# Hybrid attention layer: queries and keys transposed whole in f32 and split into two parts out of PSUM

## The chip, the cores and the metric

One core of one Trainium2 chip runs the whole layer in one launch. The metric is the device time of one execution in microseconds (us). The time before is the median of 3 runs; the profile comes from one further execution, whose own time stands beside its span below.

## What is computed

One decoder layer on x of 2048 tokens by 1024 channels, all in float32. Cut to what matters here:

```
hdn  = rmsnorm(x, norm_gain)
proj = hdn @ w_in                      # q,k,v,gate of mixer A and of mixer B
q, k = rope(rmsnorm_per_head(q)), rope(rmsnorm_per_head(k))
o_a  = banded_attention(q_a, k_a, v_a, 127, sinks)      # 8 heads, 2 key heads, window 128
o_b  = merge of three banded attentions at stride 1, 4, 16   # 8 heads
mixed = concat(o_a * silu(g_a), o_b * silu(g_b))
out  = x + mixed @ w_out
```

The scores are q·k over 64 channels per head. The gains of the per-head norm are large, so scores need nearly full float32 accuracy.

## The kernel before, in words

**Numbers in two parts.** TensorE multiplies in `float32r`, a format with a shorter mantissa than float32. So every operand x is held as a high part hi (x rounded to float32r) and a low part lo = x − hi, and a product is a sum of matmuls over parts: three for the projections (`mm3`, line 244), two for the scores (lines 590 and 591). Making the parts is elementwise work: hi is a copy on ACT with a float32r result, lo a subtraction on DVE or POOL.

**Stages.** `STAGES` lists eight passes over the sequence: four of kind B (two heads of mixer B each), two of kind A (four query heads and one key head of mixer A each) and two of kind O (half of the output columns each). Each pass goes over four blocks `sb` of 512 tokens, each block over two halves of 256 tokens, each half over two tiles `tt` of 128 tokens. Per tile, 24 matmuls of 128x384 (line 244) give queries, keys and values in a PSUM tile `pj`; per half, 24 (B) or 48 (A) of 128x256 give the gates.

**From projection to transposed queries and keys.** `norm_rope` (lines 405 to 431) squares and sums on ACT and DVE, multiplies by the rotary tables on DVE and adds on POOL (line 430); the result t1 has 128 tokens on the partitions. `norm_factors` computes the inverse norms on POOL (line 182). `norm_split` (lines 440 to 460) multiplies t1 by them on DVE (line 446) and writes a tile `hl` of both parts: high parts on ACT (lines 455, 456; the key's twice), low parts on POOL (lines 457, 458). `qk_transposes` (lines 462 to 503) then brings the heads' channels on the partitions with TensorE transposes of 128x128 float32r (lines 474, 484, 489, 490, 498) against the identity `idr`. In B a half takes ten of them in three PSUM tiles, in A twelve in four; each tile holds the high part of one head in one half of the partitions and its low part in the other, so that one matmul over 128 channels gives hi·k_hi + lo·k_hi, and a second one against `KL` (half of whose rows are zero) gives hi·k_lo. ACT copies the tiles out (lines 476, 477, 486, 492, 493, 501). In B, POOL copies the queries once more in another order (line 478) for the spill to memory that the dilated attention reads back.

**PSUM.** The transposes use the tile name `po`, which has two buffers. The same two serve the PV matmuls of the attention (lines 645, 735, 849) with their copies out (`ob` on ACT, then an addition on DVE, lines 566 to 570 and 737 to 740), the transposes of row statistics (lines 671, 877) and, in the first stage, lines 198 and 211.

**What sets the order.** A generator `proj` emits the projection; after each step the main loop emits attention steps from a queue `pending`, by cost numbers. The `finish` of a half (carry of the last keys, then `qk_transposes`) is deferred to the end of the second tile's matmuls of the next half. A scheduler then orders each engine's instructions with its own timeline, so the order in the program differs from the order in the text. Every engine runs its instructions in order: an instruction that waits holds up all behind it on that engine. DMAs are issued from SP.

**x and weights.** x arrives as `xs` and is split into `xh` (ACT, line 155) and `xl` (POOL or DVE, line 157) in groups of two 128-channel chunks; a half uses four groups, and there are `XB` = 6 buffers of each part. At a change of stage the next weights arrive as `stg` and are split on ACT (line 104) and DVE (line 105).

Of the kernel before, what the change touches and what calls it, by code (L numbers as in the profile page):

```python
# [21 lines left out]
XB = 6  # L22
# [11 lines left out]
def hybrid_layer(ctx, tc, xT, xn, x, wB, wA, wO, ng, gains, sinks, rot, masks, ident, out):  # L34
# [16 lines left out]
    idr = const.tile([128, 128], F32R, name="idr")  # L51
# [21 lines left out]
    def late_constants(part):  # L73
        if part == 0:
            nc.sync.dma_start(gt.rearrange("p a b c d -> p (a b c d)"),
                              bass.AP(tensor=gains.tensor, offset=gains.offset, ap=[[0, 128], [1, 512]]))
            return
        nc.sync.dma_start(idf, ident)
        nc.scalar.activation(idr, idf, AF.Copy)
# [166 lines left out]
    def proj(si, sb):  # L246
# [22 lines left out]
        for half in range(2):  # L269
# [66 lines left out]
            hls = norm_split(kind, nq, nk, t1s, fac)  # L336
            if si == 0 and hf < 7:
                rb_make(hf + 1)
            deferred.append(lambda half=half, hls=hls: finish(si, sb, half, hls))

    def finish(si, sb, half, hls):
# [3 lines left out]
        if half == 0 and sb > 0:  # L345
            pk, pl = K[si, sb - 1]
            for h in range(nk):
                nc.scalar.activation(KK[:, h, :, 0, :], f32(pk[:, h, :, 4, :]), AF.Copy)
            for h in range(nk):
                hs = slice(64 * h, 64 * h + 64)  # L350
                nc.scalar.activation(KL[hs, h, :, 0, :], f32(pl[hs, h, :, 4, :]), AF.Copy)
        yield from qk_transposes(si, sb, half, hls)
# [87 lines left out]
    def norm_split(kind, nq, nk, t1s, fac):  # L440
        nh = nq + nk
        n = nh * 64
        hls = []
        for tt, t1 in enumerate(t1s):
            t1v = t1[:, :n].rearrange("p (h d) -> p h d", d=64)
            nc.vector.tensor_tensor(t1v, t1v, fac[:, tt, :, None].to_broadcast([128, nh, 64]), op=OP.mult)  # L446
            hl = wk.tile([128, 11, 64], F32R, name="hl", bufs=2)
            k0 = 2 * nq
            if kind == "A":
                hi, lo = hl[:, 0:8:2, :], hl[:, 1:8:2, :]  # L450
            else:
                hi, lo = hl[:, 0:4:3, :], hl[:, 1:3, :]
            khi = hl[:, k0:k0 + 2 * nk, :].rearrange("p (h a) d -> p h a d", a=2)
            klo = hl[:, k0 + 2 * nk:k0 + 3 * nk, :]
            nc.scalar.activation(hi, t1v[:, :nq], AF.Copy)
            nc.scalar.activation(khi, t1v[:, nq:, None, :].to_broadcast([128, nk, 2, 64]), AF.Copy)
            nc.gpsimd.tensor_tensor(lo, t1v[:, :nq], f32(hi), op=OP.subtract)
            nc.gpsimd.tensor_tensor(klo, t1v[:, nq:], f32(khi[:, :, 0, :]), op=OP.subtract)
            hls.append(hl)
        return hls  # L460

    def qk_transposes(si, sb, half, hls):
        kind, _ = STAGES[si]
        KK, KL = K[si, sb]
        q = Q[si, sb]
        i0 = 2 * half

        for tt, hl in enumerate(hls):
            i = i0 + tt
            if kind == "B":  # L470
                blocks = [hl[:, 2 * b:2 * b + 2, :] for b in range(4)]
                pt = ps.tile([128, 4, 128], F32R, name="po", bufs=2)
                for b, a in enumerate(blocks):
                    nc.tensor.transpose(pt[:, b, :], a, idr)
                pv = f32(pt).rearrange("p h (r u) -> p h r u", u=32)
                nc.scalar.activation(q[0][:, :, i, :], f32(pt)[:, 0:2], AF.Copy)
                nc.scalar.activation(KK[:, :, :, i + 1, :], pv[:, 2:4], AF.Copy)
                nc.gpsimd.tensor_copy(q[1].rearrange("p h r (i u) -> p h r i u", u=32)[:, :, :, i, :],
                                      f32(q[0][:, :, i, :]).rearrange("p h (r u) -> p h r u", u=32))
                yield 230  # L480
            else:
                pt = ps.tile([128, 4, 128], F32R, name="po", bufs=2)
                for b in range(4):
                    nc.tensor.transpose(pt[:, b, :], hl[:, 2 * b:2 * b + 2, :], idr)
                for p in range(2):
                    nc.scalar.activation(q[p][:, :, i, :], f32(pt)[:, 2 * p:2 * p + 2], AF.Copy)
                yield 230
                pt = ps.tile([128, 4, 128], F32R, name="po", bufs=2)
                nc.tensor.transpose(pt[:, 0, :], hl[:, 8:10, :], idr)
                nc.tensor.transpose(pt[:64, 1, :], hl[:, 10, :], idr)  # L490
                pv = f32(pt).rearrange("p h (r u) -> p h r u", u=32)
                nc.scalar.activation(KK[:, 0, :, i + 1, :], pv[:, 0], AF.Copy)
                nc.scalar.activation(KL[:64, 0, :, i + 1, :], pv[:64, 1], AF.Copy)
                yield 110
        if kind == "B":
            pt = ps.tile([128, 2, 128], F32R, name="po", bufs=2)
            for tt, hl in enumerate(hls):
                nc.tensor.transpose(pt[:, tt, :], hl[:, 8:10, :], idr)
            for h in range(2):
                hs = slice(64 * h, 64 * h + 64)  # L500
                nc.scalar.activation(KL[hs, h, :, i0 + 1:i0 + 3, :].rearrange("p r i u -> p i r u"),
                                     f32(pt[hs]).rearrange("p i (r u) -> p i r u", u=32), AF.Copy)
            yield 110
# [60 lines left out]
    def evac_o(po, dst):  # L564
        ob = wk.tile([64, 512], F32, name="ob", bufs=1)
# [10 lines left out]
    def window_scores(si, sb, h, nb, l):  # L576
# [5 lines left out]
        for b in range(2):  # L582
            sc = ps.tile([128, 2, 256], F32, name="sc", bufs=2)
            for j in range(2):
# [4 lines left out]
                lw = KL[:, kh, :, k0:k0 + 2, :].rearrange("p r a u -> p a r u")  # L589
# [109 lines left out]
    def pair_units(si, sb, p, sc, osum, rows, final):  # L699
# [24 lines left out]
        def pv(b):  # L724
# [11 lines left out]
            ob = wk.tile([64, 512], F32, name="ob", bufs=1)  # L736
# [214 lines left out]
    pcost = {"B": 4 * 8 * 490 + 2 * 8 * 330 + 4 * 340, "A": 4 * 8 * 490 + 4 * 8 * 330 + 4 * 340, "O": 4 * 8 * 650}  # L951
# [88 lines left out]
```

## Time and profile before

| | |
|---|---|
| time, median of 3 runs | 1270.55 us (1269.44 to 1271.11) |
| profiled execution | 1271.72 us, of which the span of instructions 1269.9 us |
| mean granted TensorE clock | 0.970 |
| DVE busy | 867.5 us, 2288 instructions |
| ACT busy | 837.1 us, 2418 instructions |
| POOL busy | 685.3 us, 788 instructions |
| DMA | 220.98 MB, mean 174 GB/s |

How to read the profile's rows. A row of the grouped instructions has line, engine, operation, output<-inputs, shapes and count, then total busy us and mean ns of one, then the idle time of the engine just before these instructions and what ended most of it ("<-POOL hl L457 7.9": 7.9 us ended when POOL's line 457 had written hl). A row of the timeline has start, duration, engine, line, operation and count, and in brackets the idle time before it with what ended it. A row of the windows has the stretch, its length, the busy time of each engine (with instructions), the granted clock as a share of full speed, the DMA share and GB/s. Durations of matmuls overlap, so the pace of TensorE is read from differences of start times. PEld is the weight load that goes with each matmul.

### The profile page before, as it was taken

The numbers are of one execution on the slowest core, as the hardware profiler recorded it, in microseconds if no ns is written. First come the engines' busy times: TensorE is split into PE (matmuls) and PEld (weight loads), VectorE is DVE, ScalarE is ACT, GpSimd is POOL, SyncE is SP. The second block draws the span as 40 slices with busy tenths as digits, with TensorE's granted clock in tenths as the row PEclk, the third lists the DMA queues.
The fourth block names the chain that finished last, engine by engine and source line by source line (L and its number), as shares of the span: only waits on it lengthen the run. The fifth ranks groups of instructions, "written<-read, shape, count | busy, mean of one in ns | idle before, by whom it ended". The sixth has DMA issues, their size and how long they took to land. (4 is left out here: it accounts for less than half of the span.)

```text
span 1269.9 us, 25442 instructions
## 1 busy us (share of the span) xinstructions
PE 1179.8 (93%) x8328; PEld 1143.5 (90%) x8328; DVE 867.5 (68%) x2288; ACT 837.1 (66%) x2418; POOL 685.3 (54%) x788
## 2 busy tenths in 40 slices
PE   6898979988799898898998999999899999999899
PEld 6798979988699898898997999998799998999898
DVE  5666678776667677776877879888777868622221
ACT  6567777777668587676877767786776877513221
POOL 4876644566454755545676566673556565333122
PEclk9899989999999899898998999999899999999999
DMA  7454678776677776787866775555223235566551
GB/s 215 128 148 114 176 214 243 211 202 185 193 212 232 198 198 181 219 235 197 221 200 191 212 199 150 149 165 165 91 73 109 80 97 157 164 197 205 177 188 70
DMA packets 196883, 220.98 MB, mean 174 GB/s; under 512 B 34312, under 2 KB 143632, under 8 KB 196752
## 3 DMA queue, kind: packets, MB, share of 16 engines
q1 hardware_dynamic: 196752, 219.37, 59.2%
q8 instruction: 66, 1.08, 0.4%
q14 instruction: 65, 0.53, 0.1%
HBM read 164.44 MB, written 54.86 MB: 173 GB/s over the span
## 5 line engine op out<-in xcount | busy, mean ns | idle before, releaser
L244 PE MATMUL pj<-wh,xh 128*128 128x384 f32 (+1 forms) x1008 | 334.1, 334 | 18.6 <-ACT xh L155 6.7
L244 PE MATMUL pj<-wl,xh 128*128 128x384 f32 (+1 forms) x1008 | 334.9, 332 | 1.4 <-DVE wl L102 0.8
L244 PE MATMUL pj<-wh,xl 128*128 128x384 f32 (+1 forms) x1008 | 331.9, 331 | 1.1 <-POOL xl L157 0.8
L157 POOL TENSOR_TENSOR xl<-xs,xh 128x512 fp32r<-128x512 f32 x158 | 213.7, 1365 | 143.8 <-ACT xh L155 139.1
L155 ACT ACTIVATE xh<-xs 128x512 fp32r<-128x512 f32 x252 | 153.5, 627 | 115.8 <-PE pj L244 98.8
L244 PEld LDWEIGHTS pj<-wh,xh 128*128 128x128 f32 x1008 | 194.4, 193 | 22.4 <-ACT xh L155 7.1
L244 PEld LDWEIGHTS pj<-wl,xh 128*128 128x128 f32 x1008 | 194.6, 193 | 3.6 <-DVE wl L102 1.1
L244 PEld LDWEIGHTS pj<-wh,xl 128*128 128x128 f32 x1008 | 194.4, 193 | 3.5 <-DVE xl L157 1.3
L574 DVE TENSOR_TENSOR ptl<-pt,pth 128x512 fp32r<-128x512 f32 (+3 forms) x232 | 141.6, 619 | 42.2 <-ACT pth L573 40.2
L244 PE MATMUL pj<-xh,wgh 128*128 128x256 f32 x496 | 147.1, 297 | 10.7 <-DVE V L310 8.4
L244 PE MATMUL pj<-xh,wgl 128*128 128x256 f32 x496 | 145.3, 293 | 0.0
L244 PE MATMUL pj<-xl,wgh 128*128 128x256 f32 x496 | 144.7, 292 | 0.0
L573 ACT ACTIVATE pth<-pt 128x512 fp32r<-128x512 f32 (+3 forms) x232 | 123.1, 543 | 25.6 <-PE po L645 9.4
L430 POOL TENSOR_TENSOR t<-t,t 128x256 f32<-128x256 f32 (+1 forms) x96 | 79.2, 826 | 80.9 <-DVE t L421 57.2
L244 PEld LDWEIGHTS pj<-xh,wgh 128*128 128x128 f32 x496 | 97.7, 197 | 12.9 <-DVE V L310 5.8
L446 DVE TENSOR_TENSOR t<-t,fac 128x256 f32<-128x256 f32 (+1 forms) x96 | 76.9, 815 | 33.0 <-POOL fac L182 30.1
L244 PEld LDWEIGHTS pj<-xh,wgl 128*128 128x128 f32 x496 | 97.7, 197 | 0.8
L814 ACT ACTIVATE P<-P,scD 128x128 f32<-128x128 f32 (+3 forms) x128 | 71.6, 560 | 40.5 <-DVE scD L813 39.6
L244 PEld LDWEIGHTS pj<-xl,wgh 128*128 128x128 f32 x496 | 97.8, 197 | 0.4
L157 DVE TENSOR_TENSOR xl<-xs,xh 128x512 fp32r<-128x512 f32 x94 | 79.8, 859 | 20.2 <-ACT xh L155 19.8
L182 POOL TENSOR_TENSOR fac<-un,mhalf 128x8 f32<-128x8 f32 (+1 forms) x48 | 85.3, 1778 | 2.7
L599 ACT ACTIVATE P<-P,scA 128x256 f32<-128x256 f32 (+1 forms) x128 | 63.1, 495 | 23.4 <-DVE scA L598 23.0
(188 smaller groups left out, 3087.8 us busy)
## 6 DMA issues: line engine op xcount, KB each, us to landing
xs<-in_xT SPq DMA_DIRECT2D x94, 512.0 KB
xs<-mx SPq DMA_DIRECT2D x32, 512.0 KB
vd<-V SPq DMA_DIRECT2D x64, 128.0 KB
qd<-qc SPq DMA_DIRECT2D x32, 256.0 KB
TT<-tab SPq DMA_DIRECT2D x32, 256.0 KB
cv<-vd SPq DMA_DIRECT2D x32, 256.0 KB
cq<-qd SPq DMA_DIRECT2D x32, 256.0 KB
ck<-kd SPq DMA_DIRECT2D x64, 128.0 KB
```

The costliest lines, as they stand in the source:

```text
L155: nc.scalar.activation(h, f, AF.Copy)
L157: eng.tensor_tensor(l, f, f32(h), op=OP.subtract)
L182: nc.gpsimd.tensor_tensor(y, u, mhalf.to_broadcast([128, n]), op=OP.pow)
L244: nc.tensor.matmul(o, a, b, start=first and n == 0, stop=last and n == 2, skip_group_check=True)
L430: nc.gpsimd.tensor_tensor(t1[:, :n], t1[:, :n], t2[:, :n], op=OP.add)
L446: nc.vector.tensor_tensor(t1v, t1v, fac[:, tt, :, None].to_broadcast([128, nh, 64]), op=OP.mult)
L573: nc.scalar.activation(hi, pt, AF.Copy)
L574: nc.vector.tensor_tensor(lo, pt, f32(hi), op=OP.subtract)
L599: nc.scalar.activation(pd, pd, AF.Exp, bias=nb[i], scale=-1.0, accum_out=l[i])
L814: nc.scalar.activation(pd, pd, AF.Exp, bias=nb, scale=-1.0, accum_out=l)
```

## The change

- `hl` and `norm_split` go. `norm_scale` keeps only the DVE multiplication of t1 (line 441 of the changed kernel).
- The transposes take t1 itself, in float32 against `idf`, two heads (128 columns) at a time, two token tiles into one PSUM tile. A half of B has four transposes in one `po` tile, a half of A four of 128 columns in one tile and two of the key's 64 columns in another. `idr` goes.
- The parts are made on the way out of PSUM, on 64 partitions and 256 elements at a time: ACT copies hi, then DVE subtracts it from the PSUM tile and writes lo to the other half of the partitions. The key's hi is copied twice by ACT, its lo is one subtraction. In A the second pair of query heads is transposed after the copies of the first pair in the text, into the same tile.
- POOL's reordering copy in B stays, now two in a row per half. The carry of `KL` in A is two copies instead of one, and in A odd heads use the other plane of `KL`.
- `finish` yields once per half in B (436) and twice in A (436 and 218); the cost table `pcost` follows.
- `XB` goes from 6 to 7, and `ob` from one buffer to two.

```diff
-XB = 6
+XB = 7
...
-    def norm_split(kind, nq, nk, t1s, fac):
...
+    def norm_scale(nh, t1s, fac):
         for tt, t1 in enumerate(t1s):
...
             nc.vector.tensor_tensor(t1v, t1v, fac[:, tt, :, None].to_broadcast([128, nh, 64]), op=OP.mult)
-            hl = wk.tile([128, 11, 64], F32R, name="hl", bufs=2)
...
-            nc.scalar.activation(hi, t1v[:, :nq], AF.Copy)
-            nc.scalar.activation(khi, t1v[:, nq:, None, :].to_broadcast([128, nk, 2, 64]), AF.Copy)
-            nc.gpsimd.tensor_tensor(lo, t1v[:, :nq], f32(hi), op=OP.subtract)
-            nc.gpsimd.tensor_tensor(klo, t1v[:, nq:], f32(khi[:, :, 0, :]), op=OP.subtract)
...
+        def queries(tile, h, src):
+            a, b = (hi64, lo64) if h else (lo64, hi64)
+            o = tile[:, h, i0:i0 + 2, :]
+            nc.scalar.activation(o[a], src[a], AF.Copy)
+            nc.vector.tensor_tensor(o[b], src[a], f32(o[a]), op=OP.subtract)
+
+        if STAGES[si][0] == "B":
+            pt = ps.tile([128, 2, 2, 128], F32, name="po", bufs=2)
+            for b in range(2):
+                for tt, t1 in enumerate(t1s):
+                    nc.tensor.transpose(pt[:, b, tt, :], t1[:, 128 * b:128 * b + 128], idf)
+            for h in range(2):
+                queries(q[0], h, pt[:, 0])
+            pk = pt[:, 1].rearrange("p i (r u) -> p i r u", u=32)
+            for h, (a, b) in enumerate(((lo64, hi64), (hi64, lo64))):
+                nc.scalar.activation(keys(KK, h)[a], pk[a], AF.Copy)
+                nc.scalar.activation(keys(KK, h)[b], pk[a], AF.Copy)
+                nc.vector.tensor_tensor(keys(KL, h)[a], pk[a], f32(keys(KK, h)[a]), op=OP.subtract)
...
+        else:
+            pt = ps.tile([128, 2, 2, 128], F32, name="po", bufs=2)
+            for b in range(2):
+                for tt, t1 in enumerate(t1s):
+                    nc.tensor.transpose(pt[:, b, tt, :], t1[:, 128 * b:128 * b + 128], idf)
+                for h in range(2):
+                    queries(q[b], h, pt[:, b])
+            yield 436
+            pt = ps.tile([64, 2, 128], F32, name="po", bufs=2)
+            for tt, t1 in enumerate(t1s):
+                nc.tensor.transpose(pt[:, tt, :], t1[:, 256:320], idf)
+            pk = pt.rearrange("p i (r u) -> p i r u", u=32)
+            for a in (lo64, hi64):
+                nc.scalar.activation(keys(KK, 0)[a], pk, AF.Copy)
+            for h, a in enumerate((lo64, hi64)):
+                nc.vector.tensor_tensor(keys(KL, h)[a], pk, f32(keys(KK, 0)[lo64]), op=OP.subtract)
+            yield 218
...
-        ob = wk.tile([64, 512], F32, name="ob", bufs=1)
+        ob = wk.tile([64, 512], F32, name="ob", bufs=2)
```

How the order moves, at two places. The first is POOL in the second B stage, around the merge of the dilated attention's second quarter; `Rb` is a row of factors that comes from memory by DMA, `o1c` and `osum` the outputs that it scales, `t_` the rotated queries and keys, `qc` the reordered queries. Before:

```order
176 L899 TENSOR_TENSOR o1c<-o1c,Rb 128x512
177 L157 TENSOR_TENSOR xl<-xs,xh 128x512 x2
178 L478 CAST qc<-Q 128x8x32
179 L904 TENSOR_TENSOR osum<-osum,Rb 128x512
180 L457 TENSOR_TENSOR hl<-t_3251,hl 128x128
181 L458 TENSOR_TENSOR hl<-t_3251,hl 128x128
182 L457 TENSOR_TENSOR hl<-t_3313,hl 128x128
183 L458 TENSOR_TENSOR hl<-t_3313,hl 128x128
184 L905 TENSOR_TENSOR osum<-osum,o1c 128x512
```

The same place in the changed kernel:

```order
117 L886 TENSOR_TENSOR o1c<-o1c,Rb 128x512
118 L471 CAST qc<-Q 128x8x32 x2
119 L891 TENSOR_TENSOR osum<-osum,Rb 128x512
120 L892 TENSOR_TENSOR osum<-osum,o1c 128x512
121 L893 TENSOR_TENSOR osum<-osum,gc 128x512
122 L428 TENSOR_TENSOR t_3342<-t_3342,t_3343 128x256
```

The four subtractions that stood behind the multiplication by `Rb` are gone; the next transposes no longer need anything from POOL after the inverse norms.

The second place is TensorE in the first A stage, third half of its pass. `pt` holds softmax blocks in transposition, `sc` scores, `cq`, `ck` and `cl` the dilated attention's queries and keys. Before, one token tile's transposes, the other rows lying between them:

```order
3862 L244 MATMUL pj<-xl,wgh 128x256
3863 L489 MATMUL po<-idr,hl 128x128
3864 L490 MATMUL po<-idr,hl 64x128
3865 L484 MATMUL po<-idr,hl 128x128 x4
3866 L719 MATMUL pt<-idf,P 128x128 x4
```

The same half in the changed kernel, with the rows between its three groups of transposes cut:

```order
3870 L478 MATMUL po<-idf,t_9974 128x128
3871 L478 MATMUL po<-idf,t_10078 128x128
3872 L242 MATMUL pj<-wl,xh 128x384
...
3878 L484 MATMUL po<-idf,t_9974 64x128
3879 L484 MATMUL po<-idf,t_10078 64x128
3880 L242 MATMUL pj<-wl,xh 128x384
...
3893 L658 MATMUL po<-idf,eA 8x128
3894 L478 MATMUL po<-idf,t_9974 128x128
3895 L478 MATMUL po<-idf,t_10078 128x128
```

The second pair of query heads (rows 3894 and 3895) is transposed some twenty rows behind the first pair, and its first row waits on DVE, which reads the first pair out of the same PSUM tile.

More of the change, by code (lines that the diff above doesn't have):

```diff
@@ L50, in hybrid_layer @@
     idf = const.tile([128, 128], F32, name="idf")
-    idr = const.tile([128, 128], F32R, name="idr")
     mk = const.tile([128, 768], F32, name="mk")
@@ L78, in late_constants @@
         nc.sync.dma_start(idf, ident)
-        nc.scalar.activation(idr, idf, AF.Copy)
         nc.sync.dma_start(mk, masks)
@@ L335, in proj, with finish @@
                 nc.vector.scalar_tensor_tensor(z, e, 1.0, z, op0=OP.add, op1=OP.mult)
-            hls = norm_split(kind, nq, nk, t1s, fac)
+            norm_scale(nh, t1s, fac)
             if si == 0 and hf < 7:
                 rb_make(hf + 1)
-            deferred.append(lambda half=half, hls=hls: finish(si, sb, half, hls))
-    def finish(si, sb, half, hls):
+            deferred.append(lambda half=half, t1s=t1s: finish(si, sb, half, t1s))
+    def finish(si, sb, half, t1s):
         kind = STAGES[si][0]
@@ L348, in finish @@
                 nc.scalar.activation(KK[:, h, :, 0, :], f32(pk[:, h, :, 4, :]), AF.Copy)
-            for h in range(nk):
+            for h in range(2):
                 hs = slice(64 * h, 64 * h + 64)
                 nc.scalar.activation(KL[hs, h, :, 0, :], f32(pl[hs, h, :, 4, :]), AF.Copy)
-        yield from qk_transposes(si, sb, half, hls)
+        yield from qk_transposes(si, sb, half, t1s)
         if half == 0:
@@ L466, in qk_transposes @@
         i0 = 2 * half
[L468 to L477, printed above, removed]
+        lo64, hi64 = slice(0, 64), slice(64, 128)
@@ new lines, in keys @@
+        def keys(t, h):
+            return t[:, h, :, i0 + 1:i0 + 3, :].rearrange("p r i u -> p i r u")
+        def queries(tile, h, src):
[15 more added lines that the diff above has]
+                nc.vector.tensor_tensor(keys(KL, h)[a], pk[a], f32(keys(KK, h)[a]), op=OP.subtract)
+            for i in range(i0, i0 + 2):
@@ L478, in qk_transposes @@
                 nc.gpsimd.tensor_copy(q[1].rearrange("p h r (i u) -> p h r i u", u=32)[:, :, :, i, :],
                                       f32(q[0][:, :, i, :]).rearrange("p h (r u) -> p h r u", u=32))
[L480 to L503, printed above, removed]
+            yield 436
[4 more added lines that the diff above has]
+                    nc.tensor.transpose(pt[:, b, tt, :], t1[:, 128 * b:128 * b + 128], idf)
+                for h in range(2):
+                    queries(q[b], h, pt[:, b])
+            yield 436
+            pt = ps.tile([64, 2, 128], F32, name="po", bufs=2)
[7 more added lines that the diff above has]
+            yield 218
```

23 lines of the change are left out of this document (5 added, 18 removed).

## The prediction

> **What bounds the kernel now.** I read the busy times first, then busy time by stage, then which idle times stand before TensorE's instructions, then the timeline around some of them. The busy times, and windows cut at the stages (start; B; A; O):
>
> ```profile
> PE 1179.8 (93%) x8328; PEld 1143.5 (90%) x8328; DVE 867.5 (68%) x2288; ACT 837.1 (66%) x2418; POOL 685.3 (54%) x788
> ```
> ```profile
> 0.00:60.00 60.00, 43.47 (x237) 40.86 (x238) 38.19 (x81) 33.45 (x81) 39.32 (x53) 0.92 0.58 175
> 60.00:700.00 640.00, 586.73 (x3950) 567.82 (x3949) 461.67 (x1225) 472.60 (x1369) 371.61 (x463) 0.95 0.70 198
> 700.00:1060.00 360.00, 349.00 (x2498) 336.92 (x2498) 296.16 (x845) 265.35 (x825) 213.17 (x225) 0.99 0.45 133
> 1060.00:1270.00 210.00, 200.59 (x1645) 197.90 (x1645) 71.49 (x140) 65.67 (x147) 61.16 (x49) 1.00 0.53 170
> ```
>
> TensorE bounds every stage after the start. It idles 53 us of 640 in B (640 − 586.7) and 11 of 360 in A; DVE is the next busiest, 72% in B and 82% in A. So a change pays by the TensorE time that it removes and by the waits that it removes in B. The change touches the transposes of queries and keys; this is the idle time before them (the first column behind the bar is busy time, then the mean, then idle):
>
> ```profile
> L474 PE MATMUL po<-idr,hl 128*128 128x128 f32 x256 | 31.6, 246 | 12.8 <-POOL hl L457 7.9 <-DVE osum L570 3.7 <-ACT RB L213 1.1
> L484 PE MATMUL po<-idr,hl 128*128 128x128 f32 x128 | 15.1, 241 | 4.7 <-DVE osum L740 2.0 <-POOL hl L457 1.1 <-POOL osum L686 0.9
> L498 PE MATMUL po<-idr,hl 128*128 128x128 f32 x64 | 11.1, 252 | 7.0 <-ACT KK L477 6.4 <-DVE osum L570 0.5
> ```
>
> Together 24.5 us, of two sorts. The first is POOL's late low parts. Timeline of POOL and of TensorE at one such wait:
>
> ```profile
> 296.10 1.26 POOL L904 TENSOR_TENSOR osum<-osum,Rb 128x512 f32<-128x512 f32 x1 [4.17 <-DMA Rb<-rD]
> 297.33 0.45 POOL L457 TENSOR_TENSOR hl<-t,hl 128x128 fp32r<-128x128 f32 x1
> ```
> ```profile
> 297.83 0.36 PE L474 MATMUL po<-idr,hl 128*128 128x128 f32 x2 [1.68 <-POOL hl L457]
> ```
>
> POOL waited 4.17 us for `Rb`, the low part stood behind it, and TensorE behind that. The second sort is a PSUM buffer that comes free late. The longest, 5.46 us, lies at a change of stage; ACT's timeline ahead of it shows the cause:
>
> ```profile
> 169.60 0.69 ACT L104 ACTIVATE wgh<-stg,ngt 128x128 fp32r<-128x128 f32 x2 [1.45 <-DMA stg<-in_wB]
> ```
> ```profile
> 171.72 0.50 PE L498 MATMUL po<-idr,hl 128*128 128x128 f32 x2 [5.46 <-ACT KK L477]
> ```
>
> ACT split weights as they arrived by DMA, and the copies out of `po` stood behind. The change leaves that as it is.
>
> **The change part by part.** *Transposes.* Before: 32 halves of B with 10 and 16 of A with 12, 512 in all. Now 32 × 4 + 16 × 6 = 224. The pace of both sorts, from start times between matmuls:
>
> ```profile
> 569.85 0.60 PE L828 MATMUL pt<-idf,P 128*128 128x128 f32 x4
> 570.21 0.42 PE L244 MATMUL pj<-wh,xh 128*128 128x384 f32 x1
> 570.47 0.40 PE L808 MATMUL sc<-ck,cq 128*128 128x512 f32 x1
> ...
> 570.93 0.34 PE L244 MATMUL pj<-wl,xh 128*128 128x384 f32 x1
> 571.11 0.46 PE L474 MATMUL po<-idr,hl 128*128 128x128 f32 x4
> 571.40 0.41 PE L244 MATMUL pj<-wh,xl 128*128 128x384 f32 x1
> 571.65 0.28 PE L590 MATMUL sc<-KK,Q 128*128 128x256 f32 x1
> ```
>
> A matmul of 384 columns takes 0.18 (570.93 to 571.11). Four float32 transposes and one such matmul took 569.85 to 570.47, 0.62: 0.11 per transpose; four float32r ones and one took 571.11 to 571.65, 0.54: 0.09 each. Counted to the next start alone they are 0.09 and 0.0725. So 512 × 0.09 − 224 × 0.11 = **21.4 us** less, between 12.5 (37.1 − 24.6) and 25.9 (46.1 − 20.2). I take 21.4, since the longer count holds what the next matmul is held up. It lies on the path, because TensorE has work nearly all the time.
>
> *Low parts off POOL.* The waits released by line 457 (7.9 + 1.1 = 9.0 us) go. What is late next is t1 itself (line 446), whose factors also come from POOL behind the same `Rb`; I keep **6** of the 9 (0 to 9).
>
> *DVE.* 224 subtractions are new, on 64 partitions by 256 elements from PSUM and SBUF; 192 on POOL go. Rows of that form, of the neighbouring DVE forms, and POOL's:
>
> ```profile
> L740 DVE TENSOR_TENSOR osum<-po,ob 64x256 f32<-64x256 f32 x64 | 26.4, 413 | 3.6 <-ACT ob L737 3.1
> L446 DVE TENSOR_TENSOR t<-t,fac 128x256 f32<-128x256 f32 x64 | 54.1, 860 | 27.8 <-POOL fac L182 27.2 <-POOL t L430 0.6
> L419 DVE TENSOR_TENSOR t<-pj,TT 128x256 f32<-128x256 f32 x62 | 25.7, 415 | 4.2 <-ACT V L410 4.2
> ```
> ```profile
> L457 POOL TENSOR_TENSOR hl<-t,hl 128x128 fp32r<-128x128 f32 (+1 forms) x96 | 59.2, 617 | 31.5 <-ACT hl L455 30.0 <-PE pj L244 1.3
> L458 POOL TENSOR_TENSOR hl<-t,hl 128x128 fp32r<-128x128 f32 (+1 forms) x96 | 44.6, 465 | 1.5 <-ACT hl L456 0.9 <-PE po L849 0.6
> ```
>
> 224 × 0.413 = 92.5 us on DVE; POOL loses 103.8. The same 256 elements take 415 ns from PSUM but 860 with both inputs in SBUF. One such stretch, DVE and then POOL:
>
> ```profile
> 779.86 1.25 DVE L668 TENSOR_TENSOR eA<-eA,scA 128x8 f32<-128x8 f32 x1
> ```
> ```profile
> 779.61 1.48 POOL L157 TENSOR_TENSOR xl<-xs,xh 128x512 fp32r<-128x512 f32 x1
> ```
>
> Eight elements took 1.25 us while POOL worked, ending with it. So POOL's subtractions hold DVE up too; with them gone line 446 can win up to (860 − 415) × 64 = 28 us, and I take 10, about a third, since line 157 and others on POOL stay; it enters DVE's load, not the sum. The Trainium skill, "SBUF — State Buffer", section "Who interferes with whom", has this as a lock: a DVE instruction with two SBUF inputs and a GpSimd instruction that reads SBUF exclude each other, one with at most one SBUF input isn't concerned. By it the 224 new ones keep their 413 ns, where a price like line 446's would make them 193 us; no run here shows the new ones yet.
>
> In A, DVE gets 96 × 0.413 = 40 us on 296: 336 of 360, 93%. Does DVE at such load hold TensorE up? Three windows of A already stand there:
>
> ```profile
> 750.00:775.00 25.00, 24.43 (x176) 23.75 (x175) 23.95 (x67) 16.85 (x56) 17.29 (x19) 1.00 0.56 160
> 775.00:800.00 25.00, 24.91 (x178) 23.91 (x178) 23.84 (x71) 20.30 (x64) 18.41 (x21) 1.00 0.62 175
> 950.00:975.00 25.00, 24.31 (x172) 23.17 (x171) 23.61 (x67) 19.04 (x61) 14.16 (x14) 1.00 0.30 90
> ```
>
> DVE 95% busy, TensorE idle 1.35 us of 75: no worse than A's mean. So DVE's load alone costs nothing.
>
> *ACT.* 512 instructions go (10 and 12 per half), 288 come (6 per half), 6 more carries:
>
> ```profile
> L501 ACT ACTIVATE klz<-po 64x256 fp32r<-64x256 f32 x64 | 24.0, 376 | 3.3 <-PE po L498 2.7
> L351 ACT ACTIVATE klz<-klz 64x128 fp32r<-64x128 f32 x30 | 9.0, 302 | 0.3
> ```
>
> At 302 to 376 ns the net 218 are 66 to 82 us less. TensorE's work hides ACT's; I count 0.
>
> *The second pair in A.* Its transposes wait for DVE to have read the first pair: two copies and two subtractions, 2 × 0.376 + 2 × 0.413 = 1.6 us at the least, 16 times, 25 us uncovered. In the order some twenty rows stand between, in the place shown 14 matmuls of 384 (2.5 us) and some 1.8 us of softmax transposes and scores. Queued behind the waiting row are all later matmuls. I take **+2** (0 to +8). POOL's copy for the spill now waits for both tiles and a DVE result; it holds up `Rb`'s products, which nothing on TensorE awaits soon: 0.
>
> *XB 7, two `ob`.* The wait that a seventh buffer could take away, first in the waits, then where it reached TensorE:
>
> ```profile
> ACT xh L155 <- PE pj L244: 98.8, 62, 7.4
> ```
> ```profile
> 322.76 1.12 ACT L104 ACTIVATE wh<-stg,ngt 128x384 fp32r<-128x384 f32 x2 [5.90 <-DMA stg<-in_wB]
> 324.81 1.14 ACT L155 ACTIVATE xh<-xs 128x512 fp32r<-128x512 f32 x2
> ```
> ```profile
> 325.95 0.41 PE L244 MATMUL pj<-wh,xh 128*128 128x384 f32 x1 [4.14 <-ACT xh L155]
> ```
>
> The 98.8 us are ACT's and hidden. At 326 x stood behind weights that were late; a buffer more may let x go first: **−2** (0 to −4.1). `ob`: no TensorE wait names it, 0.
>
> *Sum.* 1271.7 (the profiled execution) − 21.4 − 6 − 2 + 2 = 1244.3; the median of the runs lies 1.2 below that execution: **1243 us**.
>
> **The rivals.** *Eaten up (1262).* A `po` buffer is held through six copies and a subtraction (6 × 0.376 + 0.413 = 2.7 us) instead of two copies, and PV waits for one. If none of the waits goes and each of the 48 halves loses 0.27 us: 1271.7 − 21.4 + 13 − 1.2 = 1262. For it: 3.7 and 2.0 us already wait for `osum`, so for `po`; against it: 96 fewer tiles pass through `po`. Chance 0.15.
>
> *Slower (1291).* DVE, 93% busy in A, answers the first pair so late that TensorE stands at the second pair. It decides the sign from 21.4 / 16 = 1.3 us per half beyond the cover of about 4 us. With 2.6 us: 1271.7 − 21.4 + 42 − 1.2 = 1291. For it: the wait is new and everything on TensorE is behind it; against: the three windows above, and A's clock of 0.99 with 11 us idle. Chance 0.13.
>
> *More (1217).* All 24.5 us before the transposes go, with the 4.1, and the clock that they cost. Windows with the 5.46 and a 3.7 us wait:
>
> ```profile
> 150.00:175.00 25.00, 19.54 (x131) 19.23 (x130) 19.97 (x45) 18.05 (x52) 13.24 (x19) 0.90 0.70 202
> 575.00:600.00 25.00, 21.28 (x144) 20.53 (x143) 16.89 (x45) 16.61 (x52) 13.79 (x16) 0.93 0.76 211
> ```
>
> (0.10 + 0.07) × 25 = 4 us: 1271.7 − 21.4 − 24.5 − 4.1 − 4 − 1.2 = 1217. Against it: the weights' DMA stays. Chance 0.08. The Trainium skill, "TensorE: Matmul & The Clock Gate", Part 1, has the clock halved after an idle window of about 3.4 us; by that only waits of this length cost clock, and the two windows agree.
>
> *Nothing (1270).* The saved work falls where TensorE waits for DMA anyway. Against it: B's 53 us of idle time are a twelfth of it. Chance 0.05.
>
> **How the numbers follow.** Forecast 0.59. From 1217 to 1266 the range takes in the forecast's own bounds (1271.7 − 12.5 + 8 − 1.2 = 1266 at the top), the eaten-up case and the large one; it leaves out 0.18. Within 0.2%, 2.5 us, a measurement of this kernel can't tell a change from none. Faster: 0.59 + 0.15 + 0.08 = 0.82; same 0.05; slower 0.13.
>
> **What would show it.** Right: some 290 fewer matmuls, and no idle time before transposes named for line 457's successor; DVE near 950 us (867.5 + 92.5 − 10) with new subtractions near 413 ns; POOL near 581. Wrong: idle time before the second pair in A above 20 us in all; B's idle time above 53 us; new subtractions near 860 ns.

## The result, and the profile after

| | median us | lowest to highest |
|---|---|---|
| before | 1269.99 | 1267.36 to 1271.11 |
| changed | 1290.40 | 1284.64 to 1292.75 |

The ratio is 1.0157 (1.0119 to 1.0195): 20 us slower, where 1243 was forecast. The rival *Slower* names nearly this time (1291), but by a wait of 42 us that measures 1.4 below, so that agreement is luck. The profiled execution took 1289.28 us with a span of 1287.5, 17.6 above that of before. Busy times of the changed kernel:

```profile
PE 1179.6 (92%) x8040; PEld 1126.3 (87%) x8040; DVE 940.6 (73%) x2512; ACT 804.6 (62%) x2199; POOL 583.7 (45%) x596
```

What the prediction said of the work came true: 288 fewer matmuls, DVE 940.6 (near 950), POOL 583.7 (near 581). Yet TensorE's busy time is what it was. The new subtractions, the multiplication that was to get cheaper, and the new transposes:

```profile
L441 DVE TENSOR_TENSOR t<-t,fac 128x256 f32<-128x256 f32 x64 | 56.2, 890 | 18.3 <-POOL fac L180 15.9 <-POOL t L428 2.0
L456 DVE TENSOR_TENSOR Q<-po,Q 64x256 fp32r<-64x256 f32 x96 | 40.5, 422 | 7.9 <-ACT Q L455 5.1
L469 DVE TENSOR_TENSOR klz<-po,KK 64x256 fp32r<-64x256 f32 x64 | 26.8, 419 | 16.8 <-ACT KK L468 15.7
```
```profile
L462 PE MATMUL po<-idf,t 128*128 128x128 f32 x128 | 21.8, 284 | 0.7 <-ACT rr L866 0.6
L478 PE MATMUL po<-idf,t 128*128 128x128 f32 x64 | 13.1, 291 | 7.8 <-DVE osum L727 5.9 <-DVE Q L456 1.4 <-ACT rr L660 0.4
L484 PE MATMUL po<-idf,t 128*64 128x128 f32 x32 | 6.5, 281 | 1.1 <-DVE qc L456 0.5 <-DVE osum L727 0.5
```

The idle time before the transposes fell from 24.5 to 9.6 us, and the second pair in A (L478) waited 1.4 us for the subtractions, not 42. So the transposes don't hold the time. B's idle time in the prediction's window is 54.1 us (640 − 585.9), hardly above its mark of 53. By stage, windows show where the time went. They are cut 4 to 8 us behind the last gate matmul of B and of A, in each kernel its own (window, length, then busy PE, PEld, DVE, ACT, POOL, then clock, DMA share, GB/s); before, then changed:

```profile
0.00:678.00 678.00, 614.04 (x4090) 594.16 (x4091) 482.88 (x1265) 490.97 (x1405) 394.69 (x495) 0.95 0.69 196
678.00:1062.00 384.00, 366.61 (x2608) 352.87 (x2607) 315.13 (x886) 282.43 (x875) 231.41 (x248) 0.98 0.47 137
1062.00:1270.00 208.00, 199.15 (x1635) 196.45 (x1633) 69.49 (x138) 63.67 (x140) 59.16 (x47) 1.00 0.54 171
```
```profile
0.00:671.00 671.00, 605.28 (x3908) 575.78 (x3909) 521.58 (x1391) 466.65 (x1278) 336.64 (x376) 0.97 0.70 199
671.00:1069.00 398.00, 369.45 (x2501) 348.64 (x2500) 348.37 (x977) 274.71 (x783) 190.31 (x178) 0.97 0.45 132
1069.00:1288.00 219.00, 204.89 (x1635) 201.87 (x1634) 70.64 (x146) 63.23 (x139) 56.76 (x44) 0.97 0.52 161
```

B gained 7 us, A lost 14 and O lost 11. Cut at the start of the last gate matmuls themselves (670.5 and 1058.2 us before, 664.2 and 1064.0 changed) it is 6, 12 and 12. O has none of the new transposes; what the change touches there is the x buffers and `ob`. The waits of ACT's x splits (line 153, 155 before, where they waited 98.8 us for TensorE and 8.3 for DMA), and of DVE's low parts behind them (19.8 before):

```profile
ACT xh L153 <- PE pj L242: 71.4, 40, 8.0
ACT xh L153 <- DMA xs<-in_xT: 67.6, 33, 6.5
ACT xh L153 <- DMA xs<-mx: 45.5, 10, 7.5
DVE xl L155 <- ACT xh L153: 82.5, 36, 7.0
```

This is the new thing: ACT stands 113 us before x splits whose bytes haven't landed. How that reaches TensorE is seen in two places. ACT in B, the load's issues on SP, and TensorE:

```profile
551.76 0.72 ACT L801 ACTIVATE P<-P,scD 128x512 f32<-128x512 f32 x1 [0.76 <-DVE scD L800]
...
555.62 0.63 ACT L153 ACTIVATE xh<-xs 128x512 fp32r<-128x512 f32 x1 [3.04 <-DMA xs<-in_xT]
556.15 0.40 ACT L332 ACTIVATE gz<-G 128x256 f32<-128x256 f32 x1
556.46 0.47 ACT L560 ACTIVATE pth<-pt 128x384 fp32r<-128x384 f32 x1
```
```profile
549.09 0.45 SPq L146 DMA_DIRECT2D xs<-in_xT  x1
553.12 0.34 SPq L146 DMA_DIRECT2D xs<-in_xT  x1
```
```profile
556.98 0.50 PE L836 MATMUL po<-pth,cv 128*128 128x256 f32 x2 [1.71 <-ACT pth L560]
```

The copy of the probabilities (L560) stands two rows behind the split, and TensorE waits for it 1.71 us. And in O:

```profile
1103.22 0.63 ACT L153 ACTIVATE xh<-xs 128x512 fp32r<-128x512 f32 x1 [6.30 <-DMA xs<-mx]
1103.75 1.06 ACT L560 ACTIVATE pth<-pt 128x512 fp32r<-128x512 f32 x2
```
```profile
1104.87 0.61 PE L722 MATMUL po<-pth,V 128*128 128x512 f32 x2 [2.67 <-ACT pth L560]
```

So the theory was (X) that the seventh x buffer moves splits in ACT's queue to where their bytes aren't there yet; the rivals were (D) that DVE's longer queue costs, and (S) that any edit of the order does.

### The profile page after: what moved, and what is told of

Read it like the earlier page. It is cut to its first block, busy times and chain, and to the rows that moved or that the text cites. A ratio compares the mean times of both kernels' runs of the same rounds, so it can differ in the third digit from the quotient of the medians.

```text
span 1287.5 us, 24606 instructions
## 1 busy us (share of the span) xinstructions
PE 1179.6 (92%) x8040; PEld 1126.3 (87%) x8040; DVE 940.6 (73%) x2512; ACT 804.6 (62%) x2199; POOL 583.7 (45%) x596
## 4 chain that ended last, share of the span: by engine, by line
PE 29%; DMA 24%; DVE 23%; ACT 11%; issue 7%; POOL 5%; SPq 2%; ACTq 0%; POOLq 0%; DVEq 0%
PE pj L242 21%; DMA xs<-in_xT 10%; DMA Rb<-rD 3%; DVE ptl L561 3%; DVE t L441 3%; DMA rD<-rr 2%; ACT P L586 2%; DVE P L585 2%; ACT xh L153 2%; DVE xl L155 2%; DVE P L800 1%; DMA stg<-in_wB 1%; ACT pth L560 1%; ACT P L801 1%; DVE Q L456 1%
## 5 line engine op out<-in xcount | busy, mean ns | idle before, releaser
L242 PE MATMUL pj<-xh,wgh 128*128 128x256 f32 x496 | 149.8, 302 | 10.7 <-DVE V L308 9.1
L242 PE MATMUL pj<-xl,wgh 128*128 128x256 f32 x496 | 147.3, 297 | 0.0
L155 DVE TENSOR_TENSOR xl<-xs,xh 128x512 fp32r<-128x512 f32 x94 | 74.8, 796 | 82.7 <-ACT xh L153 82.5
L560 ACT ACTIVATE pth<-pt 128x512 fp32r<-128x512 f32 (+3 forms) x232 | 122.1, 541 | 20.0 <-PE po L836 4.8
L242 PEld LDWEIGHTS pj<-xh,wgh 128*128 128x128 f32 x496 | 99.9, 201 | 14.7 <-ACT wgh L102 4.9
L441 DVE TENSOR_TENSOR t<-t,fac 128x256 f32<-128x256 f32 (+1 forms) x96 | 79.7, 839 | 18.7 <-POOL fac L180 15.9
L586 ACT ACTIVATE P<-P,scB 128x256 f32<-128x256 f32 (+1 forms) x128 | 63.0, 494 | 21.6 <-DVE scB L585 20.7
```

The lines of the kernel that those rows point to most:

```text
L155: eng.tensor_tensor(l, f, f32(h), op=OP.subtract)
L242: nc.tensor.matmul(o, a, b, start=first and n == 0, stop=last and n == 2, skip_group_check=True)
L560: nc.scalar.activation(hi, pt, AF.Copy)
L586: nc.scalar.activation(pd, pd, AF.Exp, bias=nb[i], scale=-1.0, accum_out=l[i])
```

## The experiments

Times are medians; each ratio is to runs of the kernel before that were taken beside it. "x parts" are the buffers of `xh` and `xl` (`XB`), "weight parts" those of the split weights (`WB`), and "PV half" is a buffer of `ob`, which holds half of a PV product. "T" stands for the changed kernel with six x parts and one PV half, the transposes' part alone.

| run | edit | us | ratio, 95% |
|---|---|---|---|
| e1_xb6 | changed, six x parts | 1262.6 | 0.9938 (0.9911–0.9964) |
| e2_ob1 | changed, one PV half | 1282.2 | 1.0108 (1.0071–1.0145) |
| e3_xb6_ob1 | T | 1257.2 | 0.9922 (0.9893–0.9950) |
| e4_pairs | changed, A's pairs together | 1277.1 | 1.0081 (1.0054–1.0107) |
| f1_early_xb7 | changed, earlier x load | 1296.1 | 1.0223 (1.0170–1.0276) |
| f2_f32t | before, transposes in f32 | 1276.9 | 1.0069 (1.0045–1.0093) |
| f3_early_xb6_ob1 | T, earlier x load | 1261.0 | 0.9926 (0.9892–0.9960) |
| f4_xs3_xb6_ob1 | T, third raw x buffer | 1266.6 | 0.9984 (0.9960–1.0007) |
| g1_third_held | changed, third split held | 1269.1 | 0.9992 (0.9972–1.0011) |
| g2_pairs_xb6_ob1 | T, A's pairs together | 1257.5 | 0.9908 (0.9879–0.9937) |
| g3_before_xb7 | before, seven x and eight weight parts | 1285.9 | 1.0125 (1.0096–1.0154) |
| g4_before_wb8 | before, eight weight parts | 1268.5 | 1.0002 (0.9976–1.0029) |
| h1_load_alone | before, 224 DVE operations more | 1288.5 | 1.0165 (1.0132–1.0198) |
| h2_load_and_hold | the same, reading `po` | 1312.9 | 1.0367 (1.0324–1.0410) |
| h3_third_xl_pool | T, third low part on POOL | 1265.6 | 0.9972 (0.9943–1.0001) |
| h4_fac_first | T, norm factors first | 1257.7 | 0.9920 (0.9890–0.9951) |
| i1_key_copy_pool | T, key copy on POOL | 1277.1 | 1.0094 (1.0057–1.0131) |
| i2_all_fixes | T, pairs, factors, key copy | 1267.0 | 1.0003 (0.9979–1.0027) |

**The change in parts.** `XB = 6`; then `ob` with `bufs=1`; then both.

> The changed kernel with six x buffers again, all else as changed. In the changed kernel's trace ACT waits 113 us for x to arrive by DMA before its x splits (8 us before the change), and DVE 82 us behind those splits (20 before). Theory X (the seventh buffer lets the splits stand so early in ACT's queue that they wait for the DMA and hold up what is behind them): 1250 to 1268 us, ACT's wait for xs by DMA back under 20 us. Theory D (the new subtractions make DVE's queue long, so that what TensorE needs from DVE comes late; the buffers don't matter): 1285 to 1295, the DMA wait may go but TensorE's idle time stays near 103 us. Theory S (any edit re-rolls the order, the waits are where chance puts them): anywhere from 1250 to 1295 with no match between the wait and the time.

> The changed kernel with one buffer for the PV half again, all else as changed. Theories X and D: 1287 to 1294, as the changed kernel, since no TensorE wait names that buffer. Theory S: off by more than 6 us in either direction.

> The transposes' part of the change alone: six x buffers and one PV-half buffer. Theory X: 1250 to 1268, as with six x buffers alone. Theory D: 1285 to 1295. Theory S: not the same as the run with six x buffers alone, though both buffers do nothing visible.

One buffer fewer takes 28 us off the changed kernel (25 with one PV half): its sign turns, and both times lie where Theory X put them. The run with one PV half alone missed X's and D's range by 5 us; 8 us off the changed kernel, it counts for S by the words written before it. The same waits with six parts:

```profile
ACT xh L153 <- PE pj L242: 101.5, 50, 9.6
ACT xh L153 <- DMA xs<-in_xT: 10.1, 3, 5.8
...
ACT xh L153 <- DMA xs<-mx: 2.0, 1, 2.0
DVE xl L155 <- ACT xh L153: 17.8, 20, 1.3
```

They are back where before had them. The chain of work that ended last (a share of the span by line) says it too; changed, then six parts:

```profile
PE pj L242 21%; DMA xs<-in_xT 10%; DMA Rb<-rD 3%; DVE ptl L561 3%; DVE t L441 3%; DMA rD<-rr 2%; ACT P L586 2%; DVE P L585 2%; ACT xh L153 2%; DVE xl L155 2%; DVE P L800 1%; DMA stg<-in_wB 1%; ACT pth L560 1%; ACT P L801 1%; DVE Q L456 1%
```
```profile
PE pj L242 35%; DVE ptl L561 3%; DVE P L585 2%; DMA Rb<-rD 2%; DMA xs<-in_xT 2%; DVE t L441 2%; DMA stg<-in_wB 2%; PE po L632 2%; DMA stg<-in_wO 1%; PE po L836 1%; DMA cl<-ld 1%; DMA stg<-in_wA 1%; DMA rD<-rr 1%; DVE G L333 1%; ACT P L586 1%
```

The x loads go from 10% of that chain to 2%. Between these two profiled executions lie 26 us (1287.5 and 1261.2): 15.5 of TensorE's idle time, and 10.8 of its busy time (1179.6 and 1168.8). The granted clock isn't the reason for the latter, since it is 0.967 with seven and 0.961 with six; what lengthens the busy time isn't shown. By the last gate matmuls 10 us lie in B, 10 in A and 6 in O. The second PV half is worth no gain that can be told: 8 us less without it beside seven parts, 5 beside six, and the intervals of each pair overlap.

**A's pairs.** The loop `for b in range(2)` is split in two, so that both pairs are transposed before the first is copied out.

> The changed kernel with both pairs of query heads in A transposed ahead of all copies, so that the second pair no longer waits for DVE. The second pair's place has 7.8 us of TensorE idle time in the changed kernel's trace (all waits at line 478). Rival of the prediction (the second pair's wait): 1250 to 1270. Theories X and D: 1282 to 1292, at most those 8 us less.

> Six x parts, one PV half, and in A both pairs of queries transposed before the first is split, so that PE need not wait for DVE between them. With seven parts this took 13 us off the changed kernel (1277 against 1290); but PE waited only some 3 us at that place, so most of the 13 should be the order's chance: 1250 to 1258 us, against 1257 without it.

With seven parts 13 us less, a time in neither range; with six nothing. So it isn't the pairs in themselves; what else the edit moves beside seven parts isn't shown. ACT's waits for x loads rose meanwhile from 113 to 139 us: the sum of these waits doesn't give the size of the loss.

**Why the seventh buffer.** With six, the third of a half's four splits takes the buffer of the first group of the half now running, which TensorE reads until near that half's end; with seven, one that is free already. The built order shows it. ACT in one half of the third B stage, six parts at the left of the bar in each row, seven at the right, rows between cut; `xh` are the four splits:

```
xh x2  L153                  | xh  L153
pth, gz, Q, P  (4 rows)      | rr  L866
KK, KK, ob, pth (4 rows)     | xh  L153
KK, KK, P, sq, V (5 rows)    | P x2, pth, gz, ob, pth, Q, P, Q
P, ob, P, sq, V (5 rows)     | xh  L153        <- the third
Q, pth, Q, pth (4 rows)      | KK, KK, pth, P, P, KK, KK, ob, pth
xh  L153         <- the third| sq, V, P, ob, sq, V, Q, pth, pth
P, P; xh  L153               | xh  L153
```

Over all 63 halves the third split stands 16 instructions of ACT earlier with seven, the others 1.1 to 1.5; the order executed in the two traces gives the same numbers. Three tests follow: load the bytes sooner, hold the split back, and do the same to the kernel before.

```
                 x_load(*nx, 0)
+                x_load(*nx, 1)
...
                 if tt == 0 and nx:
-                    x_load(*nx, 1)
```

> The changed kernel with its seven x parts, but the second load of a half's x is issued right behind the first, some 24 us sooner, so that its bytes have landed when the x splits come up on ACT. Theory X1 (the seventh buffer costs because the x splits now stand on ACT ahead of the landing of their DMA, and ACT stands there with all that is queued behind): ACT's idle time ahead of xh until a DMA of xs falls from 113 us to under 20 us and the time falls to 1258 to 1266 us. Theory X2 (the DMA wait is a symptom; with seven parts the splits are simply taken too early, ahead of score and probability work, whatever the DMA does): the DMA wait falls, but the time stays at 1280 us or more.

> The transposes' part alone (six x parts, one PV half) with the second x load issued right behind the first. In that kernel ACT stood only 13 us on DMAs of xs, so by Theory X1 there is little left to gain: 1252 to 1259 us, against 1257 without the earlier load.

Both missed, and neither tests its theory: in SP's built order 10.8 other issues still stand between the two loads, 10.9 without the edit, and in the traces of the changed kernel 14.7 us lie between them against 14.8. The loads didn't move, and yet ACT's wait for them rose to 158 us. Whether the loss comes of bytes that are late (X1) or of splits that stand too early as such (X2) stays open. A third raw buffer (`xs`, `bufs=3`) does bring them sooner, but no run has it beside seven parts.

> The transposes' part alone (six x parts, one PV half) with a third buffer for the raw x loads, so that a load need not wait until the splits of two loads earlier are done. A test of whether a spare buffer as such disturbs the order: if any buffer more lets the x splits come up too early, this is slower than 1257 us by 5 us or more; by Theory X1 it is not, since here the DMA comes sooner and not the split: 1252 to 1260 us.

It missed its range by 7 us. ACT's waits for x loads then came to 8.9 us in sum, and yet 9 us were lost against T, with 17.0 us of TensorE at `sc <- DVE scD` (6.6 in T). So Theory S has its share: a spare buffer as such can cost.

In `x_split` (`ins` is its activation, `LM[0]` the matmul issued last):

```
+        if g == 2:
+            tc.add_manual_dep(ins.ins, LM[0].ins.name, mybir.DependencyInfo(
+                mybir.DependencyClass.Sync, mybir.DependencyReason.DATA), reason="as with six")
```

> The changed kernel with all of its change, seven x parts and two PV halves among it, and one dependency more: the third x split of each half waits on ACT for the matmul that released its buffer when there were six. In the built order of ACT this split then stands where six parts put it (within one instruction on the mean), where seven alone put it 16 instructions of ACT earlier. Theory X3 (the seventh buffer costs by taking the third split of each half 16 instructions sooner, into the middle of scores and probabilities and ahead of its bytes): 1257 to 1266 us, ACT's wait for DMAs of xs back under 30 us, as with six. Theory M (what costs is not that split's place but the other splits or the memory's layout): 1277 to 1290 us, as with seven.

```profile
ACT xh L154 <- PE pj L246: 80.6, 23, 10.8
ACT xh L154 <- DMA xs<-mx: 20.7, 5, 10.0
ACT xh L154 <- DMA xs<-in_xT: 12.0, 5, 5.7
```

With seven buffers and one split held where six put it, 21 of the 28 us are back, and 80 of the 101 us of ACT's waits for x loads. It came 3 us above X3's range, and the waits at 33 us in place of under 30, so the place of the third split is most of the cause and not all; the rest lies with the other three splits, a little earlier still, or with the order's chance.

> The kernel before, with seven x parts in place of six and, to make room, eight weight parts in place of nine; it is compared with the kernel before with eight weight parts and six x parts. Its third split of a half stands 18 instructions of ACT earlier by that edit. Theory X3: 15 to 30 us slower than its partner, with over 60 us of ACT waiting for DMAs of xs. If the seventh buffer costs only together with the new transposes: within 6 us of it.

> The kernel before with eight weight parts in place of nine, the partner of the kernel before with seven x parts: 1266 to 1280 us, as the weights are split ahead only at the ends of stages.

```profile
ACT xh L155 <- DMA xs<-in_xT: 107.3, 38, 6.2
ACT xh L155 <- DMA xs<-mx: 65.2, 15, 8.8
...
DVE xl L157 <- ACT xh L155: 96.8, 40, 7.9
```

17 us slower than its partner in the kernel before, with the old transposes, and 172 us of ACT at x loads where the partner has 9: X3 named both, and the seventh buffer needs no partner. Eight weight parts alone cost nothing.

**Why the transposes' part gives 11 us and not 25.** First the price, with `F32R` and `idr` replaced by `F32` and `idf` at line 474 and its like:

> The kernel before, with its 512 small transposes of the split parts made in f32 against the f32 identity (same count, same bytes, no other change). By the prediction's 0.09 and 0.11 us each, 512 x 0.02 = 10 us slower, ratio 1.008. If f32 and f32r transposes cost the same here, under 3 us: then the whole saving of the transposes is in their number (288 fewer).

9 us over 512: 0.018 us each (0.011 to 0.023 by the interval), against 0.02. Then the load, on the kernel before, 4 per half in B and 6 in A; `dm` is read by nobody. From SBUF, and then from `po`:

```
+            for _ in range(n):
+                nc.vector.tensor_tensor(dm, m1[0:64].rearrange("p (a b) -> p a b", a=2), f32(t[0:64, :, i, :]), op=OP.subtract)
...
+                nc.vector.tensor_tensor(dm, f32(pt)[0:64, k:k + 2], f32(t[0:64, :, i, :]), op=OP.subtract)
```

> The kernel before with 224 subtractions more on DVE, where the change puts its own: 64x256, from SBUF tiles, into a tile that nobody reads, each behind ACT's copy of the transposed queries. It is DVE's new load alone, without new transposes and without a longer hold of the po buffers. By the prediction's step (DVE's load alone costs nothing): within 4 us of 1269. Theory D2 (more waits for DVE, some 16 us of PE's idle time, ate the transposes' gain): 8 to 16 us slower, with PE's waits for DVE up from 34 us to 45 us or more.

> The same 224 subtractions in the kernel before, but from the transposes' PSUM tile, so that DVE also holds the po buffer until it has read it, as in the changed kernel. If the load is what costs, as the load alone; if the hold of po costs (the prediction's rival Eaten up, 19 us), 5 us or more beyond the load alone.

The new rows of DVE, first from SBUF alone (with POOL's low parts of the keys in that run, 465 ns before), then with `po` as the one PSUM input:

```profile
L471 DVE TENSOR_TENSOR dm<-mk,Q 64x256 f32<-64x256 f32 x160 | 101.6, 635 | 5.8 <-ACT Q L481 3.6 <-ACT Q L492 0.7
L471 DVE TENSOR_TENSOR dm<-mk,qc 64x256 f32<-64x256 f32 x64 | 41.4, 647 | 1.3
L458 POOL TENSOR_TENSOR hl<-t,hl 128x128 fp32r<-128x128 f32 (+1 forms) x96 | 51.6, 537 | 2.3 <-ACT hl L456 1.9 <-DVE G L335 0.4
```
```profile
L471 DVE TENSOR_TENSOR dm<-po,Q 64x256 f32<-64x256 f32 x160 | 65.6, 410 | 7.9 <-ACT Q L481 3.8 <-ACT Q L492 2.6
L471 DVE TENSOR_TENSOR dm<-po,qc 64x256 f32<-64x256 f32 x64 | 26.2, 410 | 4.4 <-ACT qc L492 3.7
```

143 us of DVE work whose results nobody reads cost 19 us, and TensorE's waits for DVE rose from 34.4 to 46.7 us, as D2 said, though the time lies above its 8 to 16. But this load isn't the change's. In its trace the 64 subtractions that overlap no POOL instruction took 404 to 420 ns, and the 160 that do took 729 on the mean: some 51 of the 143 us (143 − 224 × 0.411) are waiting beside POOL. POOL pays too, 711.3 us busy for 685.3. The change's subtractions have one input in PSUM and take 415 to 422 ns. In that form, and holding `po`, 92 us cost 44; they hold 96 tiles here, where the change holds 64. So load costs and the hold costs, but how the 44 divide, and what either costs in the changed kernel, isn't settled. From the other side, `eng` at line 154 with `g < 3` for `g < 2`, and the factors under a priority:

> The transposes' part alone (six x parts, one PV half) with the low part of the third x split of each half made on POOL in place of DVE: DVE some 33 us less, POOL some 60 us more (to near 650). Theory D2: 1248 to 1254 us, as PE's waits for DVE fall from 50 us. If DVE's load costs nothing: 1257 us or more.

> The transposes' part alone (six x parts, one PV half) with the norm factors on POOL given priority over the merge products that stand ahead of them. DVE waited 30 us for these factors in that kernel, with scores queued behind. If this wait is what ate the gain: 1245 to 1252 us, with DVE's wait for the factors under 12 us. If it is hidden, as the waiting sits beside other work: 1254 to 1260 us.

```profile
PE pj L242 <- POOL xl L155: 16.5, 7, 4.7
PE pj L242 <- DVE V L308: 10.4, 8, 3.9
```

DVE's relief came: it was 24 us less busy, and TensorE waited for it 33.6 us in sum, not 50.1. But POOL's low parts took its place (the 16.5 above, 2.7 in T), and 8 us were lost. By the words written before it this speaks for a load that costs nothing; since one wait was exchanged for another, it decides neither way. The factors' priority changed nothing, and DVE still waited 30.7 us for them: it says only that priority doesn't move them. The last two take the second key copy (line 468) to POOL, alone and with everything that did no harm:

> The transposes' part alone (six x parts, one PV half), but in B the second copy of each key's high part is made by POOL from SBUF in place of ACT from PSUM: 64 reads of 0.38 us fewer of the held po buffers, ACT 24 us less, POOL some 30 us more. If the hold of po costs in the changed kernel too (as load and hold showed in the kernel before, 24 us beyond the load alone): 1248 to 1254 us. If not: 1255 to 1261 us, as without it (1257).

> Everything that did no harm, together: six x parts, one PV half, both pairs of A transposed ahead of their copies, the norm factors first on POOL, and the second key copy on POOL. If the pieces are worth what each showed alone (nothing measurable for pairs and factors, some 5 us for the key copies): 1247 to 1256 us.

Both missed. POOL's copies took 0.44 us each, as meant, but TensorE's waits for ACT rose from 21.6 to 35.4 us and scores now waited for POOL's keys (4.7 us). No version beat T by more than its interval; T, 0.8% under the kernel before, is the best found. The nine kernels with the new transposes and six x parts lie between 1257 and 1277 us, so a difference under some 10 us between two of them isn't read as a cause here. The seventh buffer is another matter: three pairs that differ by it alone (changed, one PV half, before) give 28, 25 and 17 us, and a fourth that differs in the PV half too (earlier load) 35, all of one sign.

## Why the prediction was wrong

**The step that failed** is "a buffer more may let x go first: −2 (0 to −4.1)". The step priced the buffer by a wait that it takes away and gave it no downside. Measured: +28 us, +17 in the kernel before. The 98.8 us that ACT spent at x splits were indeed hidden, as the text said, but they also kept the splits late; with that wait gone the third split went 16 places up in an engine that takes its instructions in order, and what stood behind it (probabilities, gates, weights in O) waited for a DMA. Whether that wait or the early place as such is what costs stays open, since no run brought the bytes sooner beside seven parts. No bound of the range had a price above nothing for this term. Without the seventh buffer and the second `ob` the change comes out at 1257, inside the range, though 14 us short of the gain that the sum gives.

**Transposes, 21.4.** The price of f32 against f32r held (0.018 for 0.02). T's busy times:

```profile
PE 1166.5 (93%) x8040; PEld 1128.0 (90%) x8040; DVE 942.8 (75%) x2512; ACT 806.0 (64%) x2199; POOL 589.9 (47%) x596
```

TensorE's busy time is 13.3 us less (1166.5 for 1179.8), near the lower bound of 12.5. By the last gate matmuls T is 14 us faster in B and 4 in A, but 6 slower in O (217.5 for 211.7), where it has no such transposes; the granted clock there is 0.98 for 1.00. The kernel before takes 216.6 us there with eight weight parts and 216.8 with its transposes in f32, both at 0.98, so these 6 us needn't be the change's doing. The clock is a rival that no run separates: T's eight runs stand at 0.962 to 0.969 (mean 0.965), the 29 of the kernel before beside them at 0.964 to 0.977 (0.970). If all of TensorE's busy time went by it, that would be some 6 of the 14 us that are missing (an estimate from these numbers).

**Low parts off POOL, 6.** These waits went, but others came: TensorE's idle time in T is 91.9 us (1258.4 − 1166.5) against 90.1 before. Summed over the rows of the waits, those for POOL fell from 18.3 to 8.3 us and those for ACT from 31.3 to 21.6, while those for DVE rose from 34.4 to 50.1.

**"So DVE's load alone costs nothing"** is a second step that failed, as far as the kernel before shows it: the load from SBUF cost 19 us there, with POOL slowed by it. What the change's own 92.5 us cost in T, no run isolates. The three windows at 95% DVE showed places where TensorE had work queued, not what happens where DVE comes late. T's window of A, cut like those above:

```profile
663.00:1047.00 384.00, 362.45 (x2502) 345.47 (x2500) 345.39 (x975) 274.25 (x785) 192.52 (x178) 0.98 0.46 137
```

That is 384 us, as before by this cut (384.1 for 387.7 by the last gate matmuls), with 96 transposes less, DVE busy for 345 us in place of 315, and TensorE idle for 21.6 in place of 17.4.

**The second pair in A, +2.** Right: 1.4 us of waiting for the subtractions. The rival *Slower* gave the sign and, by luck, the time, but not the place. *Eaten up* had a true mechanism (the hold of `po`), which the load and hold run makes visible; in T it isn't separated. The subtractions' 413 ns, DVE's 950 and POOL's 581 came out within some 2% (415 to 422 ns, 940.6 and 583.7 us). Of the 28 us that line 446 might win none came in the changed kernel (890 ns for 860), and a fifth in T (773). Its instructions still overlap POOL's work: in the changed kernel 67 of 96 do and take 1007 ns on the mean, the other 29 take 452.

## What to carry to other kernels

A buffer more is an edit of the order: before it is counted as a gain or as nothing, look at which instruction it sets free, where that now stands in its engine's queue, whether its data have landed by then, and what stands behind it. A wait that is hidden can still be what keeps an instruction from standing too early. Load on an engine below saturation is priced by adding idle load of that form, in place, in number and with its inputs in the same memories, to the kernel before, and not by windows in which nothing happened to go wrong.

## What the runs showed of the hardware

The same DVE subtraction of 64x256 took 635 to 647 ns on the mean with both inputs in SBUF and 410 with one in PSUM, in kernels where POOL is over half busy. The difference is POOL's: of the 224 with both inputs in SBUF, the 64 that overlapped no POOL instruction took 404 to 420 ns, the other 160 took 729 on the mean. With one input in PSUM it made no difference (412 ns for the 70 that overlapped none, 409 for the others). POOL was held up in turn, 537 ns for 465 at its line 458. The Trainium skill, "SBUF — State Buffer", section "Who interferes with whom", has a DVE instruction with two SBUF inputs contend with a GpSimd instruction that reads SBUF; these rows agree with it.

DVE load whose results nobody reads cost 19 us of 1269 with DVE 75% and TensorE 92% busy; POOL was slowed with it, so the 19 us aren't DVE's alone.
